# A two-layer hybrid decoder kernel: silu clamps moved to GpSimd, one norm's sums copied out of PSUM, a sum split in the tail, and three changes of order

## The chip, the cores and the metric

The kernel runs on one core of a Trainium2 chip. The metric is the device time of one execution in microseconds (us). Five engines work side by side, each through its own queue, strictly in that queue's order: PE (TensorE, matrix products and transposes), DVE (VectorE), ACT (ScalarE), POOL (GpSimd) and SP (which here only issues DMAs). An instruction starts when its engine is free and the instructions on other engines that it depends on have signalled. SBUF is the on-chip memory; PSUM is the small memory of eight banks into which PE writes.

## The reference

Two layers of a decoder trunk with 1024 channels over 528 positions (16 learned ones and 512 real ones). Each layer norms its input, projects it, runs two kinds of attention heads, projects back, adds, and then runs a gated feed-forward block. What matters here, cut from the reference:

```python
def head_groupnorm(o, g):
    mu = jnp.mean(o, axis=-1, keepdims=True)
    var = jnp.mean(jnp.square(o - mu), axis=-1, keepdims=True)
    y = (o - mu) * lax.rsqrt(var + EPS)
    ...
def hybrid_layer(h, attn_norm_g, w_in, b_fgate, ret_gn_g, w_out,
                 ffn_norm_g, w_gate, w_up, w_down, cos, sin):
    xn = rmsnorm(h, attn_norm_g)
    proj = jnp.einsum('bld,dc->blc', xn, w_in)
    fq, fk, fv, flog, rq, rk, rv, rg = jnp.split(proj, SPLIT_POINTS, axis=-1)
    ...
    fox_out = fox_attention(...)            # 8 heads of 64: softmax with a decay from flog
    ...
    ret = retention_chunkwise(rq_, rk_, rv.reshape(rshape))   # 4 heads of 128
    ret = head_groupnorm(ret, ret_gn_g).astype(h.dtype)
    ret_out = jax.nn.silu(rg) * ret
    mix = jnp.concatenate([fox_out, ret_out], axis=-1)
    h = h + jnp.einsum('blc,cd->bld', mix, w_out)
    hn = rmsnorm(h, ffn_norm_g)
    ff = jax.nn.silu(jnp.einsum('bld,df->blf', hn, w_gate)) * jnp.einsum('bld,df->blf', hn, w_up)
    return h + jnp.einsum('blf,fd->bld', ff, w_down)
```

After both layers comes one more `rmsnorm`, and the 16 learned positions are dropped.

## The kernel before, in words

**Layout and precision.** Channels lie on the 128 partitions, positions in the free dimension, so the residual stream is eight tiles `h[0..7]` of 128x528. Every product is made from high and low halves: an operand is rounded to `hi` (on ACT) and the remainder `lo` is taken by a subtraction (`split`, L150 on ACT and L151 on DVE, for activations; L199 on ACT and L202 on POOL or DVE for weights). One product is then three matmuls, hi x hi, hi x lo and lo x hi. On POOL a weight's remainder is taken in single tiles of 128x128, four for each 128x512 rounding of L199, so a run of eight L202 rows is one weight block.

**Dense products** (`dense_steps`, L225) come in *chunks*: one 128-row block of the contraction, six matmuls 264 columns wide in layer 0 (two halves of 528) or three of 512 in layer 1. Eight chunks make one 128-column block of a projection. The two inputs `xh`, `xl` of a chunk come from `scale_split` (L327 on ACT, L328 on DVE).

**Attention work** is laid between the chunks. The forgetting heads ("fox") come in pairs, each pair giving score matmuls (L524, 16 to 400 wide, the widest in two halves of 264), a maximum (L528, DVE), an exponential (L541, ACT), transposes on PE (L427), a split of the transposed weights (`pth` L150 on ACT, `ptl` L151 on DVE) and the product with the values (L586, L594), which ends in `ol` (L597, ACT) and `mixt` (L598, DVE). The four retention heads ("ret") have values (L690, L691, DVE), rotated queries and keys (`rq`, `rk`; L635 to L640), scores (L727), a decay (`sd`, L732, DVE), a split into `rsh` (ACT) and `rsl` (DVE), a product (L761, L766), a norm (`head_norm`, which calls `col_rstd`) and the silu gate.

**The gate of heads 0 and 1** (`g_done`) first evicts `sg` from PSUM (L655, DVE), then clamps it from below at -80 into `ge` (L664), and takes exp, ln, exp on ACT (L665, L666, L667). The gate is used only later, in `weigh`. The clamp therefore runs four times: heads 0 and 1 in both layers.

**`col_rstd`** sums squares over partitions with a matmul against ones (L298), into one `psa` bank per half; ACT takes ln from the banks (L303) and exp (L304), and DVE refines (L305, L307 reading the banks again, L308).

**Order.** PE's order is exactly the program's order (`manual_schedule`). It comes out of `plan`: `merge` lays lists of steps between the chunks at positions given by numbers (`m0`, `r0`, `places` for the first two groups of heads). On ACT, DVE, POOL and SP a scheduler orders the instructions by priority; `tc.high_priority()` raises it, `pin` keeps program order and `issue_after` puts one instruction behind another.

**PSUM.** Dense products use two double banks (`psd`), everything else four single banks (`psa`) in rotation: a matmul that opens a bank waits until the bank's last reader, on ACT or DVE, is done.

**The tail.** After the last down projection (L912) the last 240 positions are normed: squares `S`, `sq` (L1140, ACT), additions on DVE (`sum_b`, L1143), three fp32 matmuls of the sums against ones (L1169; the trace records each in two passes), root (L1157, ACT), three DVE steps (L1161 to L1165), four scalings (L1147) and the output DMAs.

**Feed-forward of layer 1.** `scale_split` prepares its inputs (L327, L328), and `x_forms` makes a scaled copy `S` on ACT (L873) for a few combinations.

Of the kernel before, what the change touches and what calls it, by code (L numbers as in the profile page):

```python
# [13 lines left out]
ALU = mybir.AluOpType  # L14
# [9 lines left out]
RH = 4  # L24
# [15 lines left out]
def hybrid_kernel(ctx, tc, x_t, w_in, w_fl, w_out, w_gate, w_up, w_down, vecs, b_fg, rope, decay, mask, ident, out_t):  # L40
# [250 lines left out]
    def col_rstd(parts, n, cols, rname, pinned=False):  # L291
# [7 lines left out]
        with tc.high_priority():  # L299
            r = tt(rname)  # L300
            a = tt("nwt")
            for v, (c0, c1) in zip(views, cols):
                pin(nc.scalar.activation(r[:, c0:c1], v, AF.Ln, bias=epsc, scale=1.0 / n), pinned)  # L303
            pin(nc.scalar.activation(r[:, c_all], r[:, c_all], AF.Exp, scale=-0.5), pinned)  # L304
            nc.vector.tensor_mul(a[:, c_all], r[:, c_all], r[:, c_all])  # L305
            for v, (c0, c1) in zip(views, cols):
                nc.vector.scalar_tensor_tensor(a[:, c0:c1], v, n * EPS, a[:, c0:c1], ALU.add, ALU.mult)  # L307
            nc.vector.scalar_tensor_tensor(r[:, c_all], a[:, c_all], 3.0 * n, r[:, c_all], ALU.subtract, ALU.mult)  # L308
# [10 lines left out]
    def scale_split(st, gcol, cols, then=None):  # L319
# [3 lines left out]
        for k in range(NK):  # L323
# [3 lines left out]
            pin(nc.scalar.activation(xh[:, c], h[k][:, c], AF.Copy, scale=g), then)  # L327
# [301 lines left out]
    def ret_dense(l, hd, ly, real, st, which):  # L629
# [23 lines left out]
        def g_done(ps):  # L653
# [10 lines left out]
            nc.vector.scalar_tensor_tensor(u, x, -80.0, x, ALU.max, ALU.max)  # L664
# [11 lines left out]
    def ret_steps(l, hd, st, real):  # L676
# [27 lines left out]
        def scores(grp):  # L704
# [31 lines left out]
            split(sh[:, 0:full], sl[:, 0:full], sd[:, 0:full])  # L736
# [55 lines left out]
        def head_norm():  # L792
            d = st["d"]
            r = col_rstd(st["parts"], 128, QC, "r")
            gn = tmp.tile([128, 1], F32, name="gn", tag="gn")
            nc.vector.tensor_scalar_mul(gn, vcol(V_GN + l * RH + hd), (1.0 if hd < 2 else -1.0) / 256.0)
            nc.vector.scalar_tensor_tensor(sv(d, real), sv(d, real), gn, sv(r, real), ALU.mult, ALU.mult)
# [27 lines left out]
    def ffn(l, st, real, last):  # L825
# [40 lines left out]
        def x_forms(k):  # L866
            def go():
# [5 lines left out]
                nc.scalar.activation(s[:, 0:2], two(h[k]), AF.Copy, scale=g0)  # L873
# [221 lines left out]
        else:  # L1095
# [34 lines left out]
            def square_b(m):  # L1130
                if m == 0:
                    t = fft("S", F32, (128, 6, w), 2)
                    fin["one"] = [t[:, i, 0:nb] for i in range(2)]
                    fin["acc"], fin["rb"], fin["tb"] = (t[:, i, 0:nb] for i in range(3, 6))
                    d = fin["acc"]
                elif m < NK - 2:
                    fin["sq", m] = d = tt("sq")[:, 0:nb]
                else:
                    d = fin["one"][m - NK + 2]
# [112 lines left out]
    def layer(l):  # L1252
# [188 lines left out]
```

## Time and profile before

| what | value |
|---|---|
| time, median of 3 runs | 1268.45 us (1268.43 to 1269.03) |
| the profiled execution's own time | 1268.51 us |
| its span, first to last instruction | 1266.7 us |
| PE busy | 1250.7 us (99%), 9223 matmul records |
| DVE busy | 994.4 us (79%) |
| ACT busy | 706.2 us (56%) |
| POOL busy | 274.3 us (22%) |
| mean granted TensorE clock | 0.998 |

The span is 1.8 us shorter than the execution's own time. "L664" is line 664 of the kernel before. A row of a timeline gives the start in us from the span's beginning, the duration, engine, line, operation, `out<-in`, the shapes, a count where several like instructions stand together, and in brackets how long the engine sat idle before it and which instruction ended that.

### The profile page before, as it was taken

What the parts mean: (1) busy time and instruction counts of PE and PEld (TensorE: products, weight loads), DVE (VectorE), ACT (ScalarE), POOL (GpSimd) and SP (SyncE); (2) the same over time, 40 slices, a digit from 0 to 9 for tenths busy, and PEclk for the clock granted to TensorE, in tenths of its full rate; (3) what the DMA queues carried; (4) which work ended last, traced back from release to release, by engine and by line L of the source; (5) the groups of instructions that cost most, each with busy time, mean ns of one, the idle gap of its engine ahead of it and who ended that gap; (6) DMA issues with size and microseconds to landing.
All of it is one profiled execution on the core that took longest, in us unless ns stands there. A gap on an engine that the chain in (4) does not pass through costs nothing.

```text
span 1266.7 us, 23528 instructions
## 1 busy us (share of the span) xinstructions
PE 1250.7 (99%) x9223; PEld 1192.2 (94%) x9223; DVE 994.4 (79%) x1800; ACT 706.2 (56%) x1305; POOL 274.3 (22%) x540
## 2 busy tenths in 40 slices
PE   9999999999999999999999999999999999999997
PEld 9999999999999999999999989998789999999996
DVE  8887756879988888887786877567899888888867
ACT  7767655676444444444466665557764444444445
POOL 3555546420000000000126556554100000000000
PEclk9999999999999999999999999999999999999999
DMA  6212222223333333332322122222233333333321
GB/s 218 67 60 69 83 76 73 71 67 117 105 97 100 100 101 100 101 101 84 101 77 84 61 84 74 71 89 67 100 96 121 100 101 101 100 101 101 100 84 67
DMA packets 43342, 116.19 MB, mean 92 GB/s; under 512 B 5088, under 2 KB 12000, under 8 KB 43232
## 3 DMA queue, kind: packets, MB, share of 16 engines
q1 hardware_dynamic: 42800, 114.41, 28.1%
q8 instruction: 72, 1.18, 0.4%
q14 instruction: 38, 0.31, 0.1%
q10 hardware_dynamic: 432, 0.29, 0.1%
HBM read 112.58 MB, written 2.10 MB: 91 GB/s over the span
## 4 chain that ended last, share of the span: by engine, by line
PE 91%; DVE 4%; ACT 4%; issue 1%; DMA 0%; ACTq 0%; DVEq 0%
PE psd L225 28%; PE psa L912 18%; PE psd L1047 14%; PE psd L912 13%; PE psa L225 5%; PE psa L1047 4%; PE psa L427 2%; PE psa L524 1%; PE psa L594 1%; PE psa L761 1%; PE psa L727 1%; ACT whi L199 1%; PE psa L298 0%; ACT xh L327 0%; DMA raw<-w_in 0%
## 5 line engine op out<-in xcount | busy, mean ns | idle before, releaser
L202 POOL TENSOR_TENSOR wlo<-raw,whi 128x128 fp32r<-128x128 f32 x504 | 259.1, 548 | 256.0 <-ACT whi L199 235.3
L225 PE MATMUL psd<-xh,whi 128*128 128x264 f32 (+1 forms) x792 | 195.5, 314 | 0.0
L225 PE MATMUL psd<-xh,wlo 128*128 128x264 f32 (+1 forms) x792 | 186.9, 304 | 0.0
L225 PE MATMUL psd<-xl,whi 128*128 128x264 f32 (+1 forms) x792 | 186.4, 303 | 0.4 <-DVE xl L328 0.4
L225 PEld LDWEIGHTS psd<-xh,whi 128*128 128x128 f32 x792 | 128.5, 190 | 4.9 <-ACT whi L199 0.5
L225 PEld LDWEIGHTS psd<-xh,wlo 128*128 128x128 f32 x792 | 127.0, 188 | 6.3 <-DVE wlo L202 0.4
L225 PEld LDWEIGHTS psd<-xl,whi 128*128 128x128 f32 x792 | 127.6, 189 | 5.1 <-DVE xl L328 1.1
L199 ACT CAST whi<-raw 128x512 fp32r<-128x512 f32 (+1 forms) x168 | 97.9, 613 | 41.7 <-PE psd L225 28.6
L900 ACT CAST whi<-raw 128x1024 fp32r<-128x1024 f32 (+2 forms) x62 | 54.8, 885 | 51.2 <-PE psd L912 39.8
L900 ACT CAST fwhi<-raw 128x1024 fp32r<-128x1024 f32 (+2 forms) x62 | 55.6, 897 | 48.0 <-PE psd L912 40.5
L122 POOL MEMSET kc<- 64x528 f32 x2 | 1.1, 532 | 345.4 <-PE psa L912 345.4
L901 DVE TENSOR_TENSOR wlo<-raw,whi 128x1024 fp32r<-128x1024 f32 (+2 forms) x62 | 62.9, 1015 | 12.6 <-ACT whi L900 12.5
L901 DVE TENSOR_TENSOR fwlo<-raw,fwhi 128x1024 fp32r<-128x1024 f32 (+2 forms) x62 | 64.0, 1033 | 11.0 <-ACT fwhi L900 10.7
L912 PE MATMUL psa<-th,whi 128*128 128x264 f32 (+1 forms) x232 | 65.4, 282 | 0.0
L912 PE MATMUL psa<-th,wlo 128*128 128x264 f32 (+1 forms) x232 | 65.4, 282 | 0.0
L912 PE MATMUL psa<-tl,whi 128*128 128x264 f32 (+1 forms) x232 | 65.3, 282 | 0.0
L912 PE MATMUL psa<-th,fwhi 128*128 128x264 f32 (+1 forms) x224 | 63.4, 283 | 0.0
L912 PE MATMUL psa<-tl,fwhi 128*128 128x264 f32 (+1 forms) x224 | 63.3, 283 | 0.0
L912 PE MATMUL psa<-th,fwlo 128*128 128x264 f32 (+1 forms) x224 | 63.2, 282 | 0.0
L541 ACT ACTIVATE pr<-pr,nmax 128x144 f32<-128x144 f32 (+1 forms) x64 | 36.8, 575 | 44.4 <-DVE nmax L528 25.7
L900 ACT CAST fwhi<-S 128x1024 fp32r<-128x1024 f32 x20 | 21.0, 1049 | 68.6 <-PE psa L912 66.5
L978 ACT COPY e<-psa 128x264 f32<-128x264 f32 (+1 forms) x114 | 42.9, 376 | 28.3 <-PE psa L912 24.1
(368 smaller groups left out, 4044.8 us busy)
## 6 DMA issues: line engine op xcount, KB each, us to landing
raw<-w_in SPq DMA_DIRECT2D x54, 512.0 KB, 3.5
raw<-w_gate SPq DMA_DIRECT2D x44, 512.0 KB, 4.0
fraw<-w_up SPq DMA_DIRECT2D x38, 512.0 KB, 3.5
raw<-w_down SPq DMA_DIRECT2D x64, 256.0 KB, 2.9
raw<-w_out SPq DMA_DIRECT2D x16, 512.0 KB, 3.5
raw<-w_down SPq DMA_DIRECT2D x32, 192.0 KB, 2.5
raw<-w_up SPq DMA_DIRECT2D x6, 512.0 KB, 3.5
h<-x_t SPq DMA_DIRECT2D x8, 264.0 KB, 4.5
```

The costliest lines, as they stand in the source:

```text
L199: pin(nc.scalar.copy(hi, job["raw"][:, c0:c1]), pinned)
L202: pin(sub(lo[:, c:c + step], job["raw"][:, c0 + c:c0 + c + step], hi[:, c:c + step].bitcast(F32)), pinned)
L225: nc.tensor.matmul(ps[1][b][:, 0:c1 - c0], w[:, wk, :], x[:, c0:c1], start=(k == 0 and i == 0), stop=(k == n - 1 and i == 2))
L427: nc.tensor.transpose(ps[:, 128 * j:128 * j + 128], src[:, o:o + 128], idt)
L524: nc.tensor.matmul(sc[0:nq, 0:c1 - c0], qq[:, q0:q0 + nq], kk[:, c0:c1], start=(i == 0), stop=(i == 1))
L541: nc.scalar.activation(pr, pr, AF.Exp, bias=nmax[0:nq], scale=-1.0, accum_out=rsum)
L594: nc.tensor.matmul(po[:, c0:SEQ], v[:, j, :], pp[:, j, META + c0:T], start=(j == 0 and i == 0), stop=(j == 4))
L900: nc.scalar.copy(hi, src)
L901: nc.vector.tensor_sub(lo, src, hi.bitcast(F32))
L912: nc.tensor.matmul(bank()[:, 0:b.shape[-1]], a[:, o + k, :], b, start=(fresh and k == 0 and i == 0), stop=(k == n - 1 and i == 2), skip_gr ...
L978: nc.scalar.copy(self.t["e"][:, i], self.t["x"][:, 0:w])
L1047: nc.tensor.matmul(v[:, 0:c1 - c0], a[:, s * n + k, :], b[:, c0:c1], start=(k == 0 and i == 0), stop=(k == n - 1 and i == 2))
```

## The change

Six edits, each small:

1. **Clamps.** The clamp of the gates of heads 0 and 1 (four instructions in all) goes from DVE (`scalar_tensor_tensor`, the tile given as both inputs) to POOL (`tensor_scalar_max`, one input and a constant).
2. **First heads of layer 0 later.** The first pair's main steps are spread over chunks 12 to 33 instead of 11 to 32.5, and the values of retention head 0 stand at 16.5 instead of 13. Layer 1 keeps its numbers.
3. **Sums aside.** For the third retention head (`hd == 2`) of layer 0, `col_rstd` copies the two halves of the sums from their banks into SBUF (two ACT copies, 128x264 each), and DVE's step (L307 before) then reads that copy, in one instruction of 128x528 instead of two of 128x264 from PSUM.
4. **Roundings first.** The split of the retention scores gets high priority for head 3's last group (2, 3, 4) and head 0's first group (0).
5. **Last scaling first.** In layer 1's feed-forward, each scaled copy `S` of `x_forms` is issued behind the last `xh` of `scale_split`.
6. **Tail.** The square of `h[5]` is kept as a summand of its own: the sums become four fp32 matmuls instead of three, and the DVE addition of square 5 goes.

The core of the diff:

```diff
-    def col_rstd(parts, n, cols, rname, pinned=False):
+    def col_rstd(parts, n, cols, rname, pinned=False, aside=False):
...
+            if aside:
+                t = tt("sq")
+                for v, (c0, c1) in zip(views, cols):
+                    nc.scalar.copy(t[:, c0:c1], v)
+                views, cols = [t[:, c_all]], [(cols[0][0], cols[-1][1])]
...
-            pin(nc.scalar.activation(xh[:, c], h[k][:, c], AF.Copy, scale=g), then)
+            st["scaled"] = nc.scalar.activation(xh[:, c], h[k][:, c], AF.Copy, scale=g)
+            pin(st["scaled"], then)
...
-            nc.vector.scalar_tensor_tensor(u, x, -80.0, x, ALU.max, ALU.max)
+            nc.gpsimd.tensor_scalar_max(u, x, -80.0)
...
-            split(sh[:, 0:full], sl[:, 0:full], sd[:, 0:full])
+            with tc.high_priority() if (hd, grp[0]) in ((RH - 1, 2), (0, 0)) else ExitStack():
+                split(sh[:, 0:full], sl[:, 0:full], sd[:, 0:full])
...
-            r = col_rstd(st["parts"], 128, QC, "r")
+            r = col_rstd(st["parts"], 128, QC, "r", aside=hd == 2 and not real)
...
-                nc.scalar.activation(s[:, 0:2], two(h[k]), AF.Copy, scale=g0)
+                with tc.issue_after(st["scaled"].ins) if real else ExitStack():
+                    nc.scalar.activation(s[:, 0:2], two(h[k]), AF.Copy, scale=g0)
...
-                    fin["one"] = [t[:, i, 0:nb] for i in range(2)]
+                    fin["one"] = [t[:, i, 0:nb] for i in range(3)]
...
-                elif m < NK - 2:
+                elif m < NK - 3:
...
-                sum_b(5)
...
-                sums(v, [fin["one"][0], fin["acc"], fin["one"][1]])
+                sums(v, [fin["one"][0], fin["acc"]] + fin["one"][1:])
...
-            m0, r0, places = (((7 if l else 11, 31 if l else 32.5), (34, 40.5), (13, 33.5, 35.5, 37.5, 39, 40.5, 43, 44, 47.5, 48)),
+            m0, r0, places = (((7 if l else 12, 31 if l else 33), (34, 40.5), (13 if l else 16.5, 33.5, 35.5, 37.5, 39, 40.5, 43, 44, 47.5, 48)),
```

How the order moves at three places (in the rows of the change, lines are numbered as in the changed file: L473 is L467 before, L530 is L524, L670 is the clamp, L671 to L673 are the gate's exp, ln and exp, L581 is L575).

POOL's queue in layer 1, around retention head 0. The `kc` rows belong to the first and second fox pair's keys, `wlo` are weight remainders. Before:

```order
L202 TENSOR_TENSOR wlo<-raw,whi 128x128 x32
L467 TENSOR_SCALAR kc_8391<-fs,pick 40x528
L202 TENSOR_TENSOR wlo<-raw,whi 128x128 x16
L467 TENSOR_SCALAR kc_8392<-fs,pick 40x528
L202 TENSOR_TENSOR wlo<-raw,whi 128x128 x40
```

And with the change:

```order
L473 TENSOR_SCALAR kc_8393<-fs,pick 40x528
L202 TENSOR_TENSOR wlo<-raw,whi 128x128 x16
L473 TENSOR_SCALAR kc_8394<-fs,pick 40x528
L202 TENSOR_TENSOR wlo<-raw,whi 128x128 x8
L670 TENSOR_SCALAR ge<-sg 128x512
L202 TENSOR_TENSOR wlo<-raw,whi 128x128 x32
```

The clamp stands behind a run of eight weight remainders. Head 0 of layer 0 has the same picture (behind a `kc` row and eight remainders); for head 1 the clamp stands behind one remainder in layer 0 and two in layer 1.

ACT's queue at the same place of layer 1, with the change. `whi` are the roundings that the eight remainders need, `ge` and `gr` the gate, `rsh` the rounded scores of retention head 0:

```order
L199 CAST whi<-raw 128x512 x2
L581 CAST pth<-pe 16x4x16
L671 ACTIVATE ge<-ge 128x512
L150 CAST pth<-psa 128x2x128
L672 ACTIVATE gr<-ge,onec 128x512
L150 CAST rsh<-sd 128x512
L673 ACTIVATE gr<-gr 128x512
L150 CAST pth<-psa 128x3x128
L150 CAST rsh<-sd 128x400
```

Up to L673 these rows stand as they stood before (there the exp is L665 and waited for DVE's clamp); only the last two rows have changed places.

PE's queue in layer 0 at the first score matmuls (`kc` x `qo`, 16 wide). Before:

```order
L225 MATMUL psd<-xh_181,whi 128x264 x2
L225 MATMUL psd<-xl_182,whi 128x264 x2
L225 MATMUL psd<-xh_181,wlo 128x264 x2
L524 MATMUL psa<-kc_105,qo_103 16x16
L524 MATMUL psa<-kx_462,qs_453 16x16
```

And with the change:

```order
L225 MATMUL psd<-xh_181,whi 128x264 x2
L225 MATMUL psd<-xl_182,whi 128x264 x2
L225 MATMUL psd<-xh_181,wlo 128x264 x2
L225 MATMUL psd<-xh_185,whi 128x264 x2
L225 MATMUL psd<-xl_186,whi 128x264 x2
L225 MATMUL psd<-xh_185,wlo 128x264 x2
L530 MATMUL psa<-kc_105,qo_103 16x16
L530 MATMUL psa<-kx_462,qs_453 16x16
```

One chunk more runs ahead of the first score. Further on, the five transposes of the fox values (`pd_115`) now come ahead of the five of the retention values (`pd_116`), and the latter stand behind the score 272 wide. PE has one matmul more in all (the tail's), SP's queue is the same row for row.

More of the change, by code (lines that the diff above doesn't have):

```diff
@@ L1132, in square_b @@
                     t = fft("S", F32, (128, 6, w), 2)
-                    fin["one"] = [t[:, i, 0:nb] for i in range(2)]
+                    fin["one"] = [t[:, i, 0:nb] for i in range(3)]
                     fin["acc"], fin["rb"], fin["tb"] = (t[:, i, 0:nb] for i in range(3, 6))
                     d = fin["acc"]
-                elif m < NK - 2:
+                elif m < NK - 3:
                     fin["sq", m] = d = tt("sq")[:, 0:nb]
                 else:
-                    d = fin["one"][m - NK + 2]
+                    d = fin["one"][m - NK + 3]
                 pin(nc.scalar.activation(d, h[m][:, cb], AF.Square))
```

## The prediction

> **What bounds the kernel now.** I read the page's busy shares first, then the chain that ended last.
>
> ```profile
> PE 1250.7 (99%) x9223; PEld 1192.2 (94%) x9223; DVE 994.4 (79%) x1800; ACT 706.2 (56%) x1305; POOL 274.3 (22%) x540
> PE 91%; DVE 4%; ACT 4%; issue 1%; DMA 0%; ACTq 0%; DVEq 0%
> ```
>
> PE is busy 99% of the span and is 91% of the chain. The change takes no matmul away and adds one, so everything it can win is PE waiting. The view of waits, for PE alone, says how much that is (columns: total, times, longest).
>
> ```profile
> PE psa L727 <- DVE ptl L151: 1.0, 1, 1.0
> PE psa L761 <- DVE rsl L151: 0.9, 3, 0.4
> PE psa L1169 <- ACT S L1140: 0.9, 1, 0.9
> PE psa L524 <- DVE kc L472: 0.8, 1, 0.8
> PE psa L594 <- DVE ptl L151: 0.7, 1, 0.7
> PE psa L524 <- DVE mixt L598: 0.7, 1, 0.7
> PE psa L427 <- DVE sd L732: 0.4, 1, 0.4
> PE psa L524 <- DVE sq L691: 0.4, 1, 0.4
> PE psd L225 <- DVE xl L328: 0.4, 1, 0.4
> PE psa L761 <- ACT rsh L150: 0.2, 1, 0.2
> PE psa L427 <- DVE nmax L528: 0.2, 1, 0.2
> ```
>
> These rows sum to 6.6 us, 0.5% of the time: no change of order can win more than that and the small restart loss beside each wait. A wait costs a little more than its row says: the score at 240.47 (rows in part 3) is due 0.12 us after its neighbour of 239.48 and comes 0.87 later than that, for a wait of 0.70. I count 0.16 us beside each wait that goes. The edits aim at nearly all of these waits, so the question is what they put in their place. The place to look is the clamp.
>
> ```profile
> L664 DVE SCALAR_TENSOR_TENSOR ge<-sg x4: 658/795/3722, 62.5 to 750.2; 128x528 f32<-128x528 f32 x2, 128x512 f32<-128x512 f32 x2
>   ACT ge L665: 4.5, 2
> ```
>
> Of four clamps one took 3.72 us and the shortest 0.66; ACT waited 4.5 us for two of them. The two gates of head 1 made nobody wait.
>
> **Part 1, layer 0, 36 to 71 us (edits 1, 2, 4).** The timelines of four engines there:
>
> ```profile
> 62.32 3.38 POOL L202 TENSOR_TENSOR wlo<-raw,whi 128x128 fp32r<-128x128 f32 x8
> 62.55 3.72 DVE L664 SCALAR_TENSOR_TENSOR ge<-sg 128x528 f32<-128x528 f32 x1
> 66.30 0.64 ACT L665 ACTIVATE ge<-ge 128x528 f32<-128x528 f32 x1 [3.50 <-DVE ge L664]
> 69.38 0.62 ACT L150 CAST rsh<-sd 128x528 fp32r<-128x528 f32 x1
> 70.04 0.49 PE L761 MATMUL psa<-rsh,rvh 128*128 128x512 f32 x1 [0.20 <-ACT rsh L150]
> 70.79 0.50 PE L761 MATMUL psa<-rsl,rvh 128*128 128x512 f32 x1 [0.25 <-DVE rsl L151]
> ```
>
> DVE's clamp stood while POOL ran eight weight remainders and ended just after them; `ptl`, `sd` and so PE's waits of 1.0 and 0.4 stood behind it. The Trainium skill, "SBUF — State Buffer", section "SBUF: two separate sides", describes this: a DVE instruction with two SBUF inputs and a GpSimd instruction exclude each other, and the loser blocks. The trace agrees with 3.72 against 0.66 us.
>
> A chunk of dense work is three pairs of 264-wide matmuls, 0.25 us apart, about 0.73:
>
> ```profile
> 7.77 0.41 PE L225 MATMUL psd<-xl,whi 128*128 128x264 f32 x2
> 8.02 0.40 PE L225 MATMUL psd<-xh,wlo 128*128 128x264 f32 x2
> ```
>
> In this stretch the timeline's brackets show PE waiting 0.76, 0.20, 0.43, 0.71, 0.97, 0.44, 0.20 and 0.25 us, 3.96 in all. With the change: one chunk (0.73 us) stands ahead of the first score, so 0.76 goes. The widest `ptl` comes ahead of the 400-wide maximum on DVE, so 0.71 becomes about 0.1. The clamp leaves DVE, so 0.97 and 0.44 go. The transposes and scores that were moved wait about 0.4 and 0.35 instead of 0.20 and 0.43, since they now stand behind other DVE readers of their banks. PE then comes to the first L761 at about 70.04 - 0.20 - 0.73 - 0.6 - 0.97 - 0.44 + 0.12, less 0.8 of restart losses: 66.4.
>
> There it meets the moved clamp. POOL's prices are bounded by its nearest rows, since no clamp ran on POOL:
>
> ```profile
> L467 POOL TENSOR_SCALAR kc<-fs,pick x12: 697/703/1157, 47.2 to 798.5; 40x528 fp32r<-40x528 f32 x12
> L202 POOL TENSOR_TENSOR wlo<-raw,whi x504: 448/461/2157, 22.6 to 894.7; 128x128 fp32r<-128x128 f32 x168
> ```
>
> The same kind of operation on the same length takes 0.70 (at most 1.16); a 128x128 remainder takes 0.45 and once took 2.16. I take 0.70, with 0.45 and 2.16 as ends. The eight remainders stand behind the second pair's `kc`, which follows scores that come 1.6 us earlier than now (0.73, 0.6 and two restarts): they begin at 60.7 instead of 62.32, run 3.4 to 3.7 us until 64.4, and the clamp until 65.1. ACT then runs exp, the `sums` copy, ln and `rsh`, which now goes ahead of the second exp: four instructions of about 0.6, so `rsh` is done at 67.5. PE waits 1.1 us, `rsl` follows as now (0.75 from the first L761 to the second), and the second L761 stands at 68.25 where it was at 70.79. **Gain 2.5** (1.5 if the clamp takes 1.7; 4.0 if it never delays).
>
> **Part 2, layer 1, 697 to 703 us (edits 1, 4).** Here the same move does the opposite.
>
> ```profile
> 697.43 3.97 POOL L202 TENSOR_TENSOR wlo<-raw,whi 128x128 fp32r<-128x128 f32 x8 [4.33 <-ACT whi L199]
> 696.72 1.14 ACT L199 CAST whi<-raw 128x512 fp32r<-128x512 f32 x2
> 698.29 0.67 DVE L664 SCALAR_TENSOR_TENSOR ge<-sg 128x512 f32<-128x512 f32 x1
> 699.00 0.63 ACT L665 ACTIVATE ge<-ge 128x512 f32<-128x512 f32 x1 [1.00 <-DVE ge L664]
> 700.41 0.61 ACT L150 CAST rsh<-sd 128x512 fp32r<-128x512 f32 x1
> 701.32 0.40 PE L761 MATMUL psa<-rsh,rvh 128*128 128x512 f32 x1
> 702.00 0.50 PE L761 MATMUL psa<-rsl,rvh 128*128 128x512 f32 x1 [0.28 <-DVE rsl L151]
> ```
>
> DVE's clamp was not held up here: it ended at 698.96 in the middle of POOL's run. On POOL it stands behind the eight, which begin at 697.43 when their first rounding is done and end at 700.9 (eight at the 0.42 of part 1) to 701.4. The clamp ends at 701.6 to 702.1 and ACT's exp starts there, 2.6 to 3.1 us later than at 699.00. Behind the exp, on ACT, stand `pth`, ln, and then `rsh`, which PE's first L761 needs. `rsh` ended at 701.02, 0.30 before PE used it, and `rsl` already made PE wait 0.28, so there is no slack. The second L761 moves from 702.00 by about the exp's delay, less 0.1 because `rsl` runs after POOL's burst. **Loss 2.6** (1.2 to 4.0: the last four remainders cannot start before the second rounding ends at 697.86, so 4 x 0.45 and a clamp of 0.5 put the exp at 700.2 at best; a clamp of 2.16 adds 1.4). The high priority of `rsh` doesn't help, as ACT takes its queue in order.
>
> The Trainium skill, "GPSIMD Engine Reference", section "4.1 Engine selection", speaks against the move: a maximum belongs on VectorE, GpSimd being about twice as slow with two inputs and about as fast with one. The rows here, 0.70 for one input against DVE's 0.66, agree with the second half. By the first half the clamp would take 1.3, an estimate from that page, and both stretches would lose 0.6 more.
>
> **The gates of head 1** cost nothing: only one or two remainders (0.46 each) stand ahead of POOL's clamp, and ACT, which waited for two of the four clamps now, waited for neither of these; its own earlier work hides up to about 0.4 us. If that cover went, ACT would wait what the clamp is late, with PE's L761 far enough behind.
>
> **Part 3, head 2 of layer 0 (edit 3).**
>
> ```profile
> 240.47 0.39 PE L524 MATMUL psa<-kc,qo 128*128 128x264 f32 x1 [0.70 <-DVE mixt L598]
> 239.48 0.28 PE L524 MATMUL psa<-kx,qs 128*128 128x264 f32 x1
> 242.52 0.74 ACT L541 ACTIVATE pr<-pr,nmax 128x528 f32<-128x528 f32 x1 [3.23 <-DVE nmax L533]
> L978 ACT COPY e<-psa 128x264 f32<-128x264 f32 x57 | 21.6, 380 | 14.8 <-PE psa L912 13.0
> ```
>
> The second 264-wide score waited for a bank that DVE had still to read (0.70, 0.87 with the restart). Now two copies of 0.38 on ACT free the banks. ACT has that time (it idles 3.23 us before 242.52), but `rkh` stands behind the copies, so DVE's `rkl` comes about 0.8 later; the third L727, which needs it and has half of that to spare, will wait about 0.3 of the 0.87 again. **Gain 0.6** (0.2 to 0.87).
>
> **Part 4, the rest.** Head 3's last group (its `rsl` wait is the longest of L761's three, 0.4) keeps its neighbours on ACT and DVE: nothing. In layer 1's feed-forward PE waits 0.4 for `xl` (list of waits), because two `S` stand ahead of the last `xh` on ACT, 1.33 us in the first row below; with these behind it the wait goes: **0.35** (0 to 0.5). The second row is the tail's.
>
> ```profile
> 911.04 1.33 ACT L873 ACTIVATE S<-h,vec 128x512 f32<-128x512 f32 x2
> 1257.39 1.48 PE L1169 MATMUL psa<-S,ones 128*128 128x240 f32 x6 [0.89 <-ACT S L1140]
> ```
>
> Six passes of 0.25 follow the square of `h[6]`. With `h[5]` and the accumulated sum first, four of eight run while that square is made, and four remain: 0.5 less, of which I keep **0.25** (0 to 0.45), since their order and weight loads may not pack so well.
>
> **The sum** is 2.5 + 0.6 - 2.6 + 0.35 + 0.25 = 1.1 us. Against the profiled execution, 1268.51 us (span 1266.7 and 1.8 around it, 0.06 above the median), that gives **1267.4 us**.
>
> **Rivals.** (a) *POOL is quicker than I think*: the clamp comes at its earliest in layer 1 (loss 1.2) and in time in layer 0 (gain 4.0). Then 4.0 + 0.6 - 1.2 + 0.35 + 0.25 = 4.0, 1264.5. For it: the clamp has one input, and DVE's clamp no longer competes with POOL. Against: eight remainders took 3.4 and 4.0 in the two runs shown. (b) *The later first heads do not do what they say*: the waits at 36 to 60 us only move one chunk on, and part 1 yields only what the clamp's stall hid, 1.0. Then the sum is -0.4, 1268.9. Against: the scores' `kc` is untouched, so a chunk ahead of it must cover 0.73. (c) *Slower, through the clock*:
>
> ```profile
> 1260.00:1261.00 1.00, 0.00 (x0) 0.00 (x0) 0.93 (x3) 0.91 (x3) 0.00 (x0) 0.70 1.02 347
> 1.59 4.21 PE L1283 MATMUL psa<-wide,ones 128*128 128x512 f32 x9 [1.59 <-DVE wide L62]
> ```
>
> The first row is a window of one microsecond; the figure behind the five engines is the granted clock. It fell to half about 1.5 us after PE's last matmul (which ended at 1258.87): 0.70 over 1260 to 1261 is 0.4 us at full clock and 0.6 at half. At the start, nine 512-wide matmuls took 0.47 us each, nearly twice what the pairs of part 1 take for 528 columns, and pairs come 0.25 us apart only from 7.77 on, some 6 us after the first. A wait of 2.6 us at 701 is longer than that 1.5 and than any wait now (0.97). If the clock falls in it and needs as long as at the start, half of 5.8 us is lost, 2.9: 1270.3, and 1271.2 if the clamp takes 1.16 in both places, since then each is 0.46 later. It decides from a wait of about 1.5 us on; at waits under 1 us the clock stayed at 1.00. The Trainium skill, "TensorE: Matmul & The Clock Gate", Part 1, puts the fall after an idle window of about 3.4 us; by that rule 2.6 us stays at full clock and nothing is lost. The trace's 1.5 us agrees only if the window had begun earlier.
>
> **How the numbers follow.** My forecast has a chance of 0.54, (a) 0.24, (b) 0.10, (c) 0.12. About 0.2%, 2.5 us, is what a measurement of this kernel can tell from no change. Faster by more (under 1265.9) holds (a) nearly whole and a little of the forecast's best end: 0.26. Slower by more (over 1271.0) is (c) with a slow clamp and the worst ends of part 2's price: 0.13. The rest is 0.61. The range takes in (a), the ends of the two clamp prices against each other, and (c) at its usual clamp: 1264.2 to 1270.6.
>
> **What would show it.** Right: POOL's clamp at about 701 us of 0.7 us behind eight remainders, ACT's exp there waiting 3 to 4 us for it, a new PE wait of about 2.5 us at L761, `rsh`, in layer 1; in layer 0 one of about 1 us there and none at L727. Wrong: the clamp starting among the remainders, or lasting 1.5 us; a granted clock under 1.00 after 703 us; a DVE instruction of 3 us in its place at 61 to 65 us; first scores still waiting.

## The result, and the profile after

The change takes 1270.51 us (median of 22 runs, 1268.68 to 1271.93) where the kernel before takes 1268.82 (22 runs beside them, 1268.27 to 1270.0): ratio 1.0014, interval 1.0008 to 1.002. It is slower by 0.14%. That lies inside the predicted range and inside the 0.2% called no change, but the forecast was 1.1 us faster and the change is 1.7 us slower: the direction was wrong. The profiled execution took 1270.39 us, with a span of 1268.6. Two executions of the clamp moved alone (1516 and 4349 us) and two of the kernel before (2042 and 4349 us) were far slower than the rest, whatever the kernel, and nothing here is read from them.

PE's waits after, against the eleven rows of before:

```profile
PE psa L768 <- ACT rsh L150: 3.2, 2, 2.9
PE psa L768 <- DVE rsl L151: 1.1, 4, 0.4
PE psa L733 <- DVE ptl L151: 0.9, 1, 0.9
PE psa L433 <- ACT vv L511: 0.3, 1, 0.3
PE psa L1177 <- ACT S L1148: 0.2, 1, 0.2
```

(L768 is L761 of before, L733 is L727, L433 is L427, L1177 is L1169. PE's wait of 1.6 us for its first operand, at the start, is the same in both and left out of both lists.) Eight of the eleven old waits are gone or small; one new wait of 2.9 us holds half of what is left. But the rows sum to 5.7 us, less than the 6.6 of before, and the span is 1.9 longer. A list of waits cannot show that remainder: most of it is in matmuls that ran slowly. To find it, I paired PE's matmuls of the two traces in order and followed the difference of their starts, after less before. It is -0.08 at 23 us, -1.89 at 70, -2.63 at 242, -2.02 at 259, +1.05 at the first L761 of layer 1 (701), +2.60 at 704, +2.21 at 915, +2.13 at 940; PE ends 1.84 later.

So the loss is in a few microseconds of layer 1, around 701. The timelines there, after:

```profile
698.79 1.48 POOL L670 TENSOR_SCALAR ge<-sg 128x512 f32<-128x512 f32 x1
700.31 0.63 ACT L671 ACTIVATE ge<-ge 128x512 f32<-128x512 f32 x1 [4.30 <-POOL ge L670]
701.72 0.60 ACT L150 CAST rsh<-sd 128x512 fp32r<-128x512 f32 x1
702.38 0.50 PE L768 MATMUL psa<-rsh,rvh 128*128 128x512 f32 x1 [2.90 <-ACT rsh L150]
703.10 0.79 PE L768 MATMUL psa<-rsl,rvh 128*128 128x512 f32 x1 [0.22 <-DVE rsl L151]
703.69 0.63 PE L768 MATMUL psa<-rsh,rvl 128*128 128x512 f32 x1
704.12 0.63 PE L225 MATMUL psd<-xh,whi 128*128 128x512 f32 x1
704.55 0.63 PE L225 MATMUL psd<-xl,whi 128*128 128x512 f32 x1
```

The chain is the one forecast: clamp behind the remainders, exp, `rsh`, PE. But the clamp lasts 1.48 us, not 0.70; and behind the wait 512-wide matmuls start 0.43 us apart, not 0.23. The windows of one microsecond say why (the figure behind the five engines is the granted clock):

```profile
701.00:702.00 1.00, 0.00 (x0) 0.00 (x0) 0.42 (x1) 1.00 (x3) 0.00 (x0) 1.00 0.65 262
702.00:703.00 1.00, 0.50 (x1) 0.19 (x1) 0.65 (x2) 1.00 (x3) 0.00 (x0) 0.96 0.00 0
703.00:704.00 1.00, 0.90 (x2) 0.80 (x3) 0.99 (x3) 0.66 (x2) 0.00 (x0) 0.50 0.00 0
705.00:706.00 1.00, 1.00 (x5) 0.80 (x4) 0.00 (x0) 0.00 (x0) 0.00 (x0) 0.50 0.00 0
706.00:707.00 1.00, 1.00 (x11) 1.00 (x10) 0.00 (x0) 0.51 (x1) 0.00 (x0) 0.83 0.00 0
```

The clock halves at about 702.9, when PE is already back at work, and returns at about 706.3. That costs the 1.55 us between +1.05 and +2.60.

In layer 0 the stretch from 36 to 71 us won 1.8 us, and its timelines show a stall that the forecast's sum did not have:

```profile
60.78 3.37 POOL L202 TENSOR_TENSOR wlo<-raw,whi 128x128 fp32r<-128x128 f32 x8
64.13 1.52 POOL L670 TENSOR_SCALAR ge<-sg 128x528 f32<-128x528 f32 x1
61.64 3.12 DVE L539 TENSOR_TENSOR nmax<-nmax 128x1 f32<-128x1 f32 x1
65.02 0.46 PE L733 MATMUL psa<-rqh,rkh 128*128 128x400 f32 x1 [0.92 <-DVE ptl L151]
```

DVE's clamp is gone, and the next DVE instruction with two SBUF tiles as inputs stands in its place: the minimum of two columns, usually 0.16 us, took 3.12. It ended at 64.76, 0.6 us after POOL's eight remainders (64.15) and while POOL's clamp was running. `ptl`, behind it, still makes PE wait 0.92.

Elsewhere: head 2's score wait is gone (-0.74 from 70 to 242 us), but 0.61 of it comes back by 259 us, in two places where the now earlier PE meets DVE's work, one of them the wait of this row:

```profile
257.32 0.40 PE L768 MATMUL psa<-rsl,rvh 128*128 128x272 f32 x1 [0.21 <-DVE rsl L151]
```

The `xl` wait is gone (0.4), and the tail ends 0.3 us sooner than it would have.

### The profile page after: what moved, and what is told of

The parts are those of the page before. It is cut to its first block, busy times and chain, and to the rows that moved or that the text cites. A ratio compares the mean times of both kernels' runs of the same rounds, so it can differ in the third digit from the quotient of the medians.

```text
span 1268.6 us, 23541 instructions
## 1 busy us (share of the span) xinstructions
PE 1253.1 (99%) x9225; PEld 1194.2 (94%) x9225; DVE 990.5 (78%) x1794; ACT 706.4 (56%) x1307; POOL 278.4 (22%) x544
```

## The experiments

Two theories stood against each other. **Theory 1**: all of the loss is the moved clamp, through its price on POOL, its place in POOL's queue and the clock behind the wait; the other edits win. **Rival**: the other edits lose too (the copies, the swapped order of `pth` and `rsh`, the fourth sum), or the half clock is not PE's wait's doing. Every time below stands beside runs of the kernel before on the same chip. Their medians are 1268.59 to 1268.84, so a difference between two series of runs is good to about 0.25 us.

### Clamps back on DVE

```diff
-            nc.gpsimd.tensor_scalar_max(u, x, -80.0)
+            nc.vector.scalar_tensor_tensor(u, x, -80.0, x, ALU.max, ALU.max)
```

> The change with all four clamps back on DVE. Theory 1 (the loss is layer 1's moved clamp: 2.9 us of PE wait before L768 and then about 1.5 us at half clock): the wait and the half clock go, so about 4.6 us come back, while layer 0 can lose up to 1 us, since a DVE clamp there stands again beside POOL's eight remainders: 1266 to 1267 us. Rival (the loss lies in the other edits, such as the copies aside, the swapped ptl and rsh, the fourth tail sum): at most 1 us comes back, 1269.5 or more.

Measured: 1264.86 us (1264.67 to 1265.36), ratio 0.9969 (0.9956 to 0.9981). All other edits together win 3.7 us; the moved clamps, on top of them, cost 5.65. The rival's first half is out. It is even a little better than expected, because layer 0 is not worse: at 70 us it is 2.4 us ahead of before (-2.25 against +0.17 at 23 us), the change only 1.8. DVE there:

```profile
61.86 2.54 DVE L539 TENSOR_TENSOR nmax<-nmax 128x1 f32<-128x1 f32 x1
64.52 0.69 DVE L670 SCALAR_TENSOR_TENSOR ge<-sg 128x528 f32<-128x528 f32 x1
```

The minimum stands until POOL's eight are done (64.38), and the clamp behind it runs in 0.69 us. PE's wait for `ptl` there is 0.33 us, where the change has 0.92.

### Clamps on POOL in layer 0 alone

```diff
-            nc.gpsimd.tensor_scalar_max(u, x, -80.0)
+            if real:
+                nc.vector.scalar_tensor_tensor(u, x, -80.0, x, ALU.max, ALU.max)
+            else:
+                nc.gpsimd.tensor_scalar_max(u, x, -80.0)
```

> The change with layer 1's two clamps back on DVE, layer 0's two left on POOL. Theory 1: layer 0 as in the change (1.9 us ahead of the kernel before at 70 us), layer 1 without the 2.9 us wait and without the half clock: about 1270.5 - 4.6 = 1265.9 us. Rival (the loss lies in the other edits): 1269.5 or more.

Measured: 1265.54 us (1265.27 to 1266.08), ratio 0.9975 (0.9966 to 0.9985), as theory 1 expects. Layer 1's clamps cost 1270.51 - 1265.54 = 5.0 us and layer 0's 0.7.

### Keeping PE at work during the wait

```diff
                 st["po"] = psum_a()
+                if real and hd == 0:
+                    for _ in range(8):
+                        nc.tensor.matmul(st["po"], vh[:, 0, :], vh[:, 0:4].rearrange("p j d -> p (j d)"), start=True, stop=True)
```

> The change, with eight more 512-wide matmuls of real data ahead of retention head 0's first product in layer 1; they write a bank that the product then overwrites, so they only keep PE at work for about 1.8 of the 2.9 us in which it waits for rsh. Theory 1, its clock part: with PE idle for only about 1.1 us the granted clock stays at 1.00 and the 1.5 us lost behind the wait come back: about 1268.9 us. Rival (the half clock has nothing to do with PE idling there, or the work must be dense to hold it): 1270.5 us or more, clock under 1.00 after the wait.

Measured: 1269.16 us (1268.63 to 1269.91), ratio 1.0002 (0.9993 to 1.0011): eight useless matmuls make the change 1.35 us faster. PE's first product, and the windows behind it:

```profile
702.39 0.50 PE L771 MATMUL psa<-rsh,rvh 128*128 128x512 f32 x1 [1.06 <-ACT rsh L150]
```

```profile
702.00:703.00 1.00, 0.50 (x1) 0.19 (x1) 0.63 (x2) 1.00 (x3) 0.00 (x0) 1.00 0.00 0
703.00:704.00 1.00, 0.89 (x4) 0.75 (x5) 1.00 (x3) 0.66 (x2) 0.00 (x0) 1.00 0.00 0
```

PE starts the product when it did in the change (702.39 and 702.38), but it had sat idle for 1.06 us instead of 2.90, and the clock stayed at 1.00. So the half clock is the idle PE's doing.

### The eight remainders off POOL

```diff
-        return [dense_steps(..., g > 0 or (i == 2 and not first), i == 2,
+        return [dense_steps(..., (g > 0 and (g, i) != (1, 1)) or (i == 2 and not first), i == 2,
```

> The change with one weight block's remainders (the second fox pair's key block, in both layers) taken on DVE, two of 128x512 instead of eight of 128x128 on POOL: these are the eight that stand ahead of the clamp of head 0. The clamps stay on POOL. Theory 1 (place in POOL's queue is most of it): the clamp starts when sg is there, ACT's exp in layer 1 comes about 0.8 us late instead of 3.3, PE waits under 1 us, the clock holds, and in layer 0 nothing holds DVE's nmax for 3 us: 1265 to 1266.5 us. Rival (the clamp's own 1.5 us on POOL is what costs): PE still waits 1.5 us or more in layer 1, 1268 us or more.

Measured: 1267.15 us (1266.57 to 1267.55), ratio 0.9987 (0.9978 to 0.9996). 3.4 of the 5.65 us come back with the eight gone from POOL's queue, the half clock among them (the clock stays at 1.00 in this trace); more was expected. PE still waits 1.2 us in layer 1. The clamp starts at once but lasts longer; the view of its line first, then the timelines of POOL and DVE, in layer 0 and in layer 1:

```profile
L670 POOL TENSOR_SCALAR ge<-sg x4: 1486/1996/2768, 62.0 to 749.8; 128x528 f32<-128x528 f32 x2, 128x512 f32<-128x512 f32 x2
```

```profile
62.01 2.77 POOL L670 TENSOR_SCALAR ge<-sg 128x528 f32<-128x528 f32 x1 [0.99 <-DVE nmax L539]
62.11 1.27 DVE L202 TENSOR_TENSOR wlo<-raw,whi 128x512 fp32r<-128x512 f32 x2
695.96 2.46 POOL L670 TENSOR_SCALAR ge<-sg 128x512 f32<-128x512 f32 x1 [5.03 <-DVE sg L661]
695.79 1.27 DVE L202 TENSOR_TENSOR wlo<-raw,whi 128x512 fp32r<-128x512 f32 x2
```

In layer 0 the two remainders on DVE took 1.27 us together and the clamp 2.77, which is its 1.5 plus those 1.27; in layer 1 it took 2.46. The exclusion works in both directions: here POOL lost. Both theories hold in part: the eight on POOL are worth 3.4 us; the other 2.3 are the clamp's price on POOL and its stand beside the remainders on DVE, which this run does not separate.

### The clamp moved alone, in the kernel before

```diff
-            nc.vector.scalar_tensor_tensor(u, x, -80.0, x, ALU.max, ALU.max)
+            nc.gpsimd.tensor_scalar_max(u, x, -80.0)
```

> The kernel before with nothing changed but the four clamps on POOL. Theory 1 (the clamp on POOL is what makes the change slower): layer 1 loses the same 4.6 us (a wait of about 2.9 and the half clock behind it); in layer 0, where the clamp now stands ahead of the eight remainders, PE's waits for ptl and sd behind DVE's clamp shrink by about 1 us: 1271.5 to 1272.5 us. Rival (only the clamp together with the other edits is slow): 1270 us or less.

Measured: 1270.73 us (nine runs, 1269.18 to 1271.74), ratio 1.0014 (1.0005 to 1.0024): slower as expected, but between the two theories' figures. The starts' difference tells why: layer 1 loses 4.6 us exactly as in the change (3.05 at the wait, 1.60 behind it), but layer 0 wins 2.4, not 1. There, in the old order of steps, the clamp came ahead of the eight remainders, and DVE's column minimum took 0.30 us:

```profile
62.45 1.52 POOL L664 TENSOR_SCALAR ge<-sg 128x528 f32<-128x528 f32 x1
63.95 3.39 POOL L202 TENSOR_TENSOR wlo<-raw,whi 128x128 fp32r<-128x128 f32 x8
62.78 0.30 DVE L533 TENSOR_TENSOR nmax<-nmax 128x1 f32<-128x1 f32 x1
```

So the clamp on POOL alone wins 2.4 us in layer 0, the other edits alone win 2.4 there too (the first experiment), and both together win 1.8: they do not add.

### What POOL holds up on DVE

```diff
-                nc.vector.tensor_tensor(nmax, mins[0], mins[1], ALU.min)
+                nc.vector.tensor_scalar(nmax, mins[0], mins[1], None, ALU.min)
```

This on top of the clamps on DVE:

> The change with clamps on DVE, and the minimum of two 128x1 columns (L539) written as a tensor_scalar with the second column as its per-partition scalar instead of a tensor_tensor of two SBUF tiles. It stood 2.54 us beside POOL's eight remainders in the run with the clamps on DVE. Theory A (what POOL holds up is a DVE instruction with two SBUF tiles as inputs, and the next such one takes the place): L539 takes 0.15 us, and the clamp behind it, which has two, stands about 2.5 to 3.3 us instead; PE's wait for ptl stays: 1264.5 to 1265.5 us. Theory B (what is held up is whatever comes first while POOL runs, one input or two): L539 still stands. Theory C (the stand comes from POOL's first remainder of the run only): neither stands and 0.6 us are won, 1264.2 us.

Measured: 1264.86 us (1264.59 to 1265.61), ratio 0.9971 (0.996 to 0.9982). DVE's rows are those of theory A:

```profile
62.55 0.20 DVE L539 TENSOR_SCALAR nmax<-nmax 128x1 f32<-128x1 f32 x1
62.67 2.97 DVE L670 SCALAR_TENSOR_TENSOR ge<-sg 128x528 f32<-128x528 f32 x1
```

The stand passes to the next instruction, the clamp. And with the clamp on DVE written with one tile too (`nc.vector.tensor_scalar_max(u, x, -80.0)`):

> As the run before it, and the clamp on DVE too written with one tile as input (tensor_scalar_max). Theory A: neither L539 nor the clamp stands while POOL runs its eight; ptl comes some 2 us earlier, and PE's waits for ptl (0.3) and rsh (0.3) in layer 0 go: 1264.1 to 1264.4 us, 0.5 us under the run with the clamps on DVE. Theory B: the clamp or L539 stands 2.5 us or more, 1264.9 us or more.

Measured: 1264.79 us (1264.35 to 1265.01), ratio 0.9969 (0.9957 to 0.9981), no gain. The clamp's line, and its first execution in the timeline:

```profile
L670 DVE TENSOR_SCALAR ge<-sg x4: 383/532/2691, 61.4 to 746.7; 128x528 f32<-128x528 f32 x2, 128x512 f32<-128x512 f32 x2
```

```profile
61.43 2.69 DVE L670 TENSOR_SCALAR ge<-sg 128x528 f32<-128x528 f32 x1
```

Theory A is wrong as stated: a clamp with one input stands too. But it is another kind of instruction: undisturbed it takes 0.38 us, where the two-input form takes 0.66. The Trainium skill, "SBUF — State Buffer", section "SBUF: two separate sides", names both kinds, instructions with two SBUF inputs and those in DVE's two-port fast mode, as the ones that exclude GpSimd; the trace agrees for the 2.97 and the 2.69, and the column minimum with one input, 0.20 beside POOL's run, was free. What no run shows is why DVE loses to a whole run of eight here, while the kernel before's clamp at 698.29 took 0.67 in the middle of such a run. There POOL lost: its remainder of 698.27 took 1.03 us, where the others of that run took 0.46.

### The price of the clamp on POOL

The first price list stood at the start of layer 0's feed-forward:

```diff
+                for _ in range(2):
+                    for p, w in ((128, T), (128, HALF), (64, T), (40, T)):
+                        nc.gpsimd.tensor_scalar_max(s[0:p, 0:w], h[0][0:p, 0:w], -80.0)
+                    nc.gpsimd.tensor_scalar(s[0:40], h[0][0:40], pick[:, 0:1], 0.0, ALU.mult, ALU.add)
...
```

> The kernel before with sixteen extra POOL instructions at the start of layer 0's feed-forward, where POOL is otherwise idle; they write a tile that nobody reads. Twice each: maximum with a constant on 128x528, 128x264, 64x528 and 40x528; the kc form (column scalar times, plus 0) on 40x528 and on 128x528; times a constant on 128x528; a subtraction of two tiles on 128x528. Theory 1 (the clamp's 1.5 us is its price undisturbed, set by the number of partitions: POOL's kc row was cheap because it has 40): maximum 1.5 on 128, about 0.75 on 64 and on 40 partitions, the kc form 1.5 on 128 partitions. Rival (the maximum itself is slow, or the price goes by the length of the row alone): the kc form takes 0.7 on 128 partitions as on 40, or the maximum takes 1.5 on 40 too.

Inconclusive: DVE was busy there, and the same instruction took 1.25 us once and 2.22 the other time. (One run, 1273.04 us.) The second list stood ahead of layer 1's first clamp, with DVE and ACT made to stand behind it:

```diff
+            if real and hd == 0:
+                for _ in range(2):
+                    nc.gpsimd.tensor_scalar_max(u, x, -80.0)
+                    nc.gpsimd.tensor_scalar_max(u.bitcast(F32R), x, -80.0)
+                    nc.gpsimd.tensor_scalar_max(u[0:40], x[0:40], -80.0)
+                    nc.gpsimd.tensor_scalar(u[0:40], x[0:40], pick[:, 0:1], 0.0, ALU.mult, ALU.add)
+                    nc.gpsimd.tensor_scalar(u[0:40].bitcast(F32R), x[0:40], pick[:, 0:1], 0.0, ALU.mult, ALU.add)
+                    nc.gpsimd.tensor_scalar_mul(u, x, 0.5)
+                    nc.gpsimd.tensor_sub(u, x, sv(msk, real))
+                    nc.gpsimd.tensor_scalar_max(u[:, 0:256], x[:, 0:256], -80.0)
```

> The change with sixteen extra POOL instructions ahead of layer 1's first clamp, on the clamp's own tiles, which the clamp overwrites; ACT, and behind it DVE and PE, stand until they are done, so nothing disturbs POOL. Twice each: maximum 128x512 to float32 and to the rounded float32 kind that kc has; maximum 40x512; the kc form (times a column, plus 0) on 40x512, to both kinds; times a constant 128x512; a subtraction of two tiles 128x512; maximum 128x256. Theory P (the price goes by elements per partition and by the two kinds of output or operation, not by partitions): 40 partitions cost what 128 do, 1.5, and the kc form or kind shows 0.7. Rival (by partitions): 40x512 costs half or less of 128x512 in the same form. 16 times about 1.2 us make the run about 15 us longer than the change.

Measured (one run, 1283.81 us); durations of each line, least, median and most in ns: maximum on 128 and on 40 partitions, kc's form, and the product with a constant.

```profile
L672 POOL TENSOR_SCALAR ge<-sg x2: 1483/1485/1487, 699.2 to 709.7; 128x512 f32<-128x512 f32 x2
L674 POOL TENSOR_SCALAR ge<-sg x2: 1477/1478/1479, 702.3 to 712.8; 40x512 f32<-40x512 f32 x2
L676 POOL TENSOR_SCALAR ge<-sg,pick x2: 685/686/687, 705.1 to 715.2; 40x512 fp32r<-40x512 f32 x2
L677 POOL TENSOR_SCALAR ge<-sg x2: 1493/1494/1496, 705.8 to 716.0; 128x512 f32<-128x512 f32 x2
```

Partitions make no difference (1.48 on 40 as on 128), and a product with a constant is as slow as a maximum. (`kc`'s form with a plain float32 result, not shown, took 0.69 once and 1.05 the other time; why is open.) So kc's row was cheap by its form. Which part of the form, the third list asks:

```diff
+                    nc.gpsimd.tensor_scalar(u, x, onec, None, ALU.max)
+                    nc.gpsimd.tensor_scalar(u, x, onec, 0.0, ALU.max, ALU.add)
+                    nc.gpsimd.tensor_scalar(u, x, onec, 0.0, ALU.mult, ALU.add)
+                    nc.gpsimd.tensor_scalar(u, x, onec, None, ALU.mult)
+                    nc.gpsimd.tensor_scalar(u, x, 0.5, 0.0, ALU.mult, ALU.add)
+                    nc.gpsimd.tensor_scalar(u, x, -80.0, 0.0, ALU.max, ALU.add)
```

> The change with twelve extra POOL instructions ahead of layer 1's first clamp, on the clamp's own tiles (128x512, float32), which the clamp overwrites; the other engines stand meanwhile. Twice each: maximum with a column; maximum with a column, then plus 0; times a column, plus 0 (kc's form); times a column; times a constant, plus 0; maximum with a constant, plus 0. The run before showed 1.48 us for a maximum and for a product with a constant, and 0.69 for kc's form, on 40 partitions as on 128. Theory K (a constant operand is what is slow): all four column forms take 0.7, both constant forms 1.5. Theory S (a second operation makes it fast): the forms with plus 0 take 0.7, the others 1.5. Theory M (the pair of multiplication and addition alone is fast): only kc's form, and perhaps a constant times plus 0, take 0.7.

Measured (one run, 1282.78 us), the six in the diff's order are L672 to L677; four of them:

```profile
L673 POOL TENSOR_SCALAR ge<-sg,onec x2: 2000/2001/2002, 701.1 to 710.1; 128x512 f32<-128x512 f32 x2
L674 POOL TENSOR_SCALAR ge<-sg,onec x2: 696/698/699, 703.2 to 712.2; 128x512 f32<-128x512 f32 x2
L675 POOL TENSOR_SCALAR ge<-sg,onec x2: 1572/1574/1576, 704.0 to 712.9; 128x512 f32<-128x512 f32 x2
L676 POOL TENSOR_SCALAR ge<-sg x2: 620/621/622, 705.7 to 714.6; 128x512 f32<-128x512 f32 x2
```

Theory M: only a product followed by an addition takes 0.6 to 0.7 us. A single operation takes 1.5 to 1.57, a maximum followed by an addition 1.93 to 2.0, with a column or a constant alike.

### The change with the price that the forecast took

The clamping is left out here; POOL's instruction only copies, at 0.62 us.

```diff
-            nc.gpsimd.tensor_scalar_max(u, x, -80.0)
+            nc.gpsimd.tensor_scalar(u, x, 1.0, 0.0, ALU.mult, ALU.add)
```

> The change with POOL's clamp replaced by a product with 1 plus 0, the form that takes 0.62 us on POOL; the clamping itself is left out. This gives the change the price that the forecast took. If only the price was mis-sized, layer 1's wait before L768 is 2.9 - 0.87 = 2.0 us, layer 0 comes out as before or 0.3 us better, and the time is 1270.5 - 0.9 = 1269.6 us with the half clock still there, or 1268.1 us if the clock holds through 2.0 us. The forecast's own figure, 1267.4 us, needs besides that the stretch of layer 0 gives 2.5 us; if DVE's nmax stands there as it did, it will not.

Measured: 1269.84 us (11 runs, 1267.89 to 1270.62), ratio 1.0007 (0.9998 to 1.0016). The profiled execution is the one of 1268.18. PE's first product, and a window behind it:

```profile
701.63 0.50 PE L768 MATMUL psa<-rsh,rvh 128*128 128x512 f32 x1 [2.07 <-ACT rsh L150]
```

```profile
703.00:704.00 1.00, 1.00 (x9) 0.81 (x7) 0.83 (x2) 0.35 (x1) 0.00 (x0) 1.00 0.00 0
```

The wait is 2.07 us, as computed, and here the clock held. Two of the eleven runs lie at 1267.89 and 1268.18, the other nine between 1269.55 and 1270.62: both expected figures, 1268.1 and 1269.6, turn up, the higher more often. That the nine are runs in which the clock fell is inferred from the 1.5 us between the groups, since only one execution has a trace.

### Two of the other edits undone

On top of the clamps on DVE, first without the copies aside:

```diff
-            r = col_rstd(st["parts"], 128, QC, "r", aside=hd == 2 and not real)
+            r = col_rstd(st["parts"], 128, QC, "r")
```

> The change with clamps on DVE and without the two copies aside (edit 3 undone). In the change, 0.8 us were won at 240 us and about 0.6 of them lost again by 259 us, where two small waits (ptl, rsl) appeared. Theory 1 (what was lost again belongs to edit 3, since its faster PE meets the next DVE work sooner): undoing it costs the difference only, 0.2 us, so 1265.1 us. Rival (the two later waits have another cause): undoing it costs the whole 0.8, 1265.7 us.

Measured: 1265.34 us (1264.8 to 1265.69), ratio 0.9973 (0.9962 to 0.9983). By the medians edit 3 is worth 0.5 us, halfway between the two figures, with ranges that overlap: not settled by the times. The traces settle it for its own stretch, 235 to 262 us. With edit 3 (the run with the clamps on DVE) the difference of PE's starts against the kernel before goes from -2.21 to -2.38 there; without edit 3 it stays at -1.84. So the edit is worth 0.17 us at its place, and both waits that follow it are its own, as theory 1 says. Where the rest of the 0.5 comes from is open; the two traces differ by 0.36 us at 23 us already, where nothing was changed. PE's row without the edit:

```profile
PE psa L530 <- DVE mixt L604: 0.7, 1, 0.7
```

Then with the first heads of layer 0 at their old places:

```diff
-            m0, r0, places = (((7 if l else 12, 31 if l else 33), (34, 40.5), (13 if l else 16.5, ...
+            m0, r0, places = (((7 if l else 11, 31 if l else 32.5), (34, 40.5), (13, ...
```

> The change with clamps on DVE and the first heads of layer 0 back at their old places (edit 2 undone). By the change's trace, edit 2 was worth the waits at 37.6 (0.76) and 58.3 us (0.71) with their restarts, less 0.1 new ones: 1.6 us by 60 us. Theory 1: they come back, 1266.4 us. Rival (they would in part be hidden again further on, where PE waits for the stretch's DVE work at L733 and L768 anyway): 1265.5 us or less.

Measured: 1267.43 us (1266.98 to 1268.27), ratio 0.9991 (0.9982 to 1.0). Edit 2 is worth 2.6 us, more than either expectation: every wait of the kernel before in this stretch is back, those behind the stand on DVE too:

```profile
PE psa L733 <- DVE ptl L151: 1.0, 1, 1.0
PE psa L530 <- DVE kc L478: 0.8, 1, 0.8
PE psa L433 <- DVE sd L738: 0.4, 1, 0.4
```

So the later heads also win what I had credited to the clamp's move.

### A version that beats both

Clamps on DVE, and in layer 0 alone the eight remainders on DVE:

```diff
-        return [dense_steps(..., g > 0 or (i == 2 and not first), i == 2,
+        return [dense_steps(..., (g > 0 and (l, g, i) != (0, 1, 1)) or (i == 2 and not first), i == 2,
```

> The change with clamps on DVE and, in layer 0 alone, the eight remainders of the second pair's key block taken on DVE in two of 128x512. If POOL's run of eight is what holds DVE's nmax for 2.5 us and then PE at L733 and L768, both waits (0.3 each, with restarts 0.9) go: 1264.0 us, the lowest of all. Rival (DVE has no room for 1.3 us more there, and its sd and rsl come later instead): 1264.9 us or more.

Measured: 1263.5 us (1263.08 to 1265.28), ratio 0.9962 (0.9949 to 0.9976), the lowest median of all, 5 us under the kernel before. Against the run with the clamps on DVE (1264.86) the ranges touch, but counted from 23 us PE is 1.4 us further ahead at 71 us (-3.86 against -2.42). The minimum no longer stands, and no PE wait at L733 is left:

```profile
61.71 0.14 DVE L539 TENSOR_TENSOR nmax<-nmax 128x1 f32<-128x1 f32 x1
```

## Why the prediction was wrong

**The bound** held: PE's waits were all that could be won, and the other edits won 3.7 us of the 6.6 and their restarts (clamps on DVE); the best version won 5.1.

**Part 2 is the step that failed.** Its loss, forecast at 2.6 us, measured 4.6, by two terms: the clamp's price, and the clock, which the sum put at nothing. The chain was right to the instruction: POOL's queue, exp, `rsh`, L761, and a loss with its sign. The forecast took the clamp at 0.70 us from kc's row as "the same kind of operation on the same length". It was 1.48; the row shared opcode and length, not the pair of operations that makes it fast. At PE the loss was 3.1, and with an instruction of 0.62 us 2.3 (the starts' difference goes from -1.93 to +0.38 there): the price is worth 0.8, and at its own price the forecast was 0.3 too high. The upper end of the bounds, 2.16 from the longest remainder, held the true price; the lower row was chosen because it was alike by name.

**The clock was a rival and should have been the forecast's companion.** It stood at 0.12 with 2.9 us; it came in 21 of 22 runs of the change, if the one at 1268.68 is the one without, and cost 1.55, since it lasted 3.4 us and not 5.8. With the fill in the wait it went, so that it comes from the idle PE is shown. Together: -2.6 forecast, -4.6 measured; without these 2.0 us the change would have been 0.3 us faster than the kernel before instead of 1.7 slower. The Trainium skill, "TensorE: Matmul & The Clock Gate", Part 1, speaks of an idle window of about 3.4 us; a fall after 2.90 of idling, and most likely after 2.07, is earlier than that. It also calls the window free-running, and the traces agree: in the change the clock rises at 6.60 us, halves at 702.92 and rises again at 706.33, which is 204 steps and one step of 3.413 us, and in every other trace too the changes of the clock lie whole numbers of this step apart. That fits a fall that varies from run to run, since it counts where among the steps a wait falls. In the change PE worked 0.50 us of the step that ended at 702.92. With the cheap instruction a step's end at 701.19 cut the wait of 2.07 in two; PE worked 1.78 us in the one step and 2.75 in the other, and the clock held. How little work is too little stays open: after PE's last matmul the clock fell behind a step with 1.48 us of work (before) and held behind one with 1.43 (after).

**Part 1** forecast 2.5 and got 1.8. The dense chunk ahead of the first score and the earlier `ptl` did as worked out. Wrong was "The clamp leaves DVE, so 0.97 and 0.44 go": the 0.44 went, but of the 0.97 there is 0.92 left, since POOL's eight took the next DVE instruction instead, as the prediction's last paragraph had named as a sign, without a price. (The wait for `rsh` behind it, forecast at 1.1, is 0.29.) And its attribution was wrong: with edit 2 and no moved clamp the stretch wins 2.4, with the moved clamp and no edit 2 it wins 2.4, with both 1.8.

**With price alone put right** (POOL's instruction at 0.62 us) the kernel is at 1268.2 while the clock holds: 0.8 over the forecast's 1267.4, which is part 1's 0.7 and the 0.5 that part 3 fell short, less the 0.3 of layer 1 and some small gains. But its median is 1269.84, not faster than before: the forecast's sign needs the clock to hold as well.

**Part 3** forecast 0.6: 0.74 at its place, 0.13 left seventeen microseconds later in the change; undoing it cost 0.17 at its place and 0.5 by the medians. **Part 4**: `xl` 0.35 forecast, 0.4 measured; tail 0.25 forecast, 0.3 measured; head 3's wait unchanged, as forecast. Rivals (a) and (b) did not occur.

## What to carry to other kernels

A duration is borrowed from a row of the same operation, not of the same opcode; if the trace has none, keep the far end of the bounds as likely as the near one when a stage has no slack. Before an in-order engine gets a job that others wait for, read what stands ahead of it there at that moment, place by place: the same move won in one layer and lost in the other. And a wait of two or three microseconds on PE is not priced by its length alone, since the clock behind it can add half as much again (1.55 us behind 2.90 here).

## What the runs showed of the hardware

- On POOL a product followed by an addition on 128x512 takes 0.62 to 0.70 us; a single maximum or product takes 1.48 to 1.57, a maximum followed by an addition 1.93 to 2.0. Forty partitions cost what 128 do.
- DVE and POOL shut each other out in both directions: a 128x1 minimum on DVE took 3.12 us beside eight remainders on POOL, POOL's clamp took 2.77 beside 1.27 us of remainders on DVE, and a remainder on POOL took 1.03 instead of 0.46 beside DVE's clamp (the kernel before, 698.27).
- The granted clock changed only at steps of 3.413 us, counted from its first rise. So it fell between 1.5 us (the kernel before: 1258.88 and 1260.41) and 5.4 us (the change: 1260.72 and 1266.12) after PE's last matmul, and in the wait of layer 1 only after PE had started again; there it stayed at half for one step, 3.41 us. It held through 1.06 us of idling in one trace and through 2.07 in another.
